# Expert scores of a mixture layer: one slab of each pair from whole float32 operands, the other in three passes

## The chip, the cores and the metric

The kernel runs on one core of a Trainium2 chip. Its time is the device time of one execution in microseconds; the figure quoted is the median of several runs. Engines are named as in the profile: PE is TensorE (PEld its weight loads), DVE is VectorE, ACT is ScalarE, POOL is GpSimd, and SP is SyncE, which issues the loads.

## The reference, cut to what matters

Two model blocks run one after the other, each with two layers, over 256 tokens of width 1024. The change lies in one part of the first block, the PEER layer, which runs once in each of its two layers: 16,384 experts, each one row of `u` and one row of `v`, of which every token takes 16 for each of 8 heads.

```python
def peer(xn, w_q, sub_keys, u, v):
    q = (xt @ w_q).astype(jnp.float32).reshape(t, PEER_HEADS, 2, PEER_HALF)
    sc = jnp.einsum('thpc,pnc->thpn', q, sub_keys.astype(jnp.float32))
    top_s, top_i = lax.top_k(sc, PEER_TOPK)
    cand = top_s[:, :, 0, :, None] + top_s[:, :, 1, None, :]
    best_s, best_c = lax.top_k(cand.reshape(t, PEER_HEADS, PEER_TOPK * PEER_TOPK), PEER_TOPK)
...
    expert = i1 * N_KEYS + i2
    gate = jax.nn.softmax(best_s, axis=-1)
...
        act = jax.nn.gelu(jnp.einsum('cd,chkd->chk', xc, u[ec]))
        return jnp.einsum('chk,chkd->cd', (gc * act).astype(xc.dtype), v[ec])
```

## The kernel before

`peer` (from L686) does not gather. It scores all 16,384 experts against all 256 tokens, multiplies by a gate that is zero for every expert not chosen, and sums the rows of `v`. The matrix `u` is streamed in 64 pairs of 256 rows; a pair is one raw tile of 1 MB, fetched by four loads of 256 KB that SP issues (`u_rows`), and has two slabs of 128 experts. DVE transposes a slab in blocks of 32 x 32, and PE multiplies it with the normalized tokens `xs` (eight tiles of 128 x 256).

There are two ways to multiply. In `u_whole` a slab is transposed out of the raw tile into a tile `ut` (L894) and multiplied as float32 in 8 products (L898; each leaves two records in the trace). In `u_split` it is transposed in place (L906); ACT copies a rounded half `whi` (L909), DVE subtracts it to get the rest `wlo` (L910), and `mm3` makes three passes for each of the 8 products (L198 to L200): high by high, high by low, low by high, with `xh` and `xl`, the halves of `xs`.

The order of the program is this. After two heads' scores, pair 0 is whole. Then a loop emits, for each pair, first the next pair's `u_whole`, then the gelu of the pair in hand (`u_out`), then four or five steps of other work: first `routing` (77 steps, nine a head, so two pairs a head), which computes the scores of heads 2 to 7 (product L762, whose weights are a further raw tile, and L772), finds the best 16 of each (L747 to L751, L789), adds up candidates (L800) and picks indices (L803, with POOL); then `spread_gates` (64 steps, 16 pairs), which turns the chosen experts and gates into a dense gate: DVE makes a one-hot `oh` (L859), `eq` (L861) and `rhs` (L863) for four tokens, PE multiplies them (L868), DVE or ACT puts the result into `act` (L872). After 37 whole pairs a layer come the other 27, as `u_split`, interleaved with the 64 pairs of `v`.

A scheduler sets the order on each engine by priority. `K.ahead()`, which is `high_priority(offset=600)`, moves what stands in it, here loads and transposes, forward in that order. Three kinds of ring tile matter, with three buffers each: `raw` (the loads of `u`, of the query weights and of `v` share it), `whi` and `wlo`. In `u_whole` the two `ut` tiles of a pair take one buffer of `whi` and one of `wlo`.

Of the kernel before, what the change touches and what calls it, by code (L numbers as in the profile page):

```python
# [12 lines left out]
F32 = mybir.dt.float32  # L13
F32R = mybir.dt.float32r
# [10 lines left out]
S = 256  # L25
KT = 8
# [642 lines left out]
def steps(gen, n):  # L669
    for _ in range(n):  # L670
        if next(gen, None) is None and gen.gi_frame is None:
            return
# [13 lines left out]
def peer(K, a, l, pre, xg, row, pool, ctx):  # L686
# [8 lines left out]
    tc, nc = K.tc, K.nc  # L695
# [36 lines left out]
    rrow = scratch([128, S])  # L732
    with tc.high_priority(offset=URGENT):
        nc.scalar.activation(rrow, row, AF.Copy)
    xs = Tiles([K.x_tile(KT + m, F32) for m in range(KT)])
    for m in range(KT):
        nc.vector.tensor_tensor(xs[:, m], xg[:, m], rrow, ALU.mult)
    skT = scratch([128, 2, 128])
# [2 lines left out]
    ps = K.ax_ps()  # L741
# [11 lines left out]
    def head_scores(hd):  # L753
        qs, sc = qs_b[hd % 2], sc_b[hd % 2]
        with K.ahead():
            raw = K.raw_tile().rearrange("p (k f) -> p k f", k=KT)
            K.rows_in(raw, a["w_peer_q"][l][:, hd * 256:hd * 256 + 256])
        x = xg if hd < 2 else xs
        ps = K.ax_ps().rearrange("p (m t) -> p m t", m=2)
        for k in range(KT):  # L760
            for m in range(2):
                nc.tensor.matmul(ps[:, m], raw[:, k, m * 128:m * 128 + 128], x[:, k], start=k + m == 0,  # L762
                                 stop=k == KT - 1 and m == 1)
        if hd < 2:
            nc.vector.tensor_tensor(qs, ps, rrow[:, None, :].to_broadcast([128, 2, S]), ALU.mult)
        else:
            nc.scalar.activation(qs, ps, AF.Copy)
        p2 = K.ax_ps()
        for tb in range(2):
            for s in range(2):  # L770
                i = 2 * tb + s
                nc.tensor.matmul(p2[:, i * 128:i * 128 + 128], qs[:, s, tb * 128:tb * 128 + 128],  # L772
                                 skT[:, s], start=True, stop=True)
        nc.scalar.activation(sc, p2.rearrange("p (i n) -> p i n", i=4), AF.Copy)
# [71 lines left out]
    def spread_gates():  # L846

        for i, t0 in enumerate(range(0, S, GT)):
            tag = "gab"[i % 3]
            pg = K.g_ps() if tag == "g" else K.ax_ps(tag)
            pg = pg.rearrange("p (t n) -> p t n", n=128)
            ts = slice(t0, t0 + GT)
            tok = lambda x: x[:, None, ts].to_broadcast([128, 128, GT])
            oh = pool.tile([128, 128, GT], FP16, name="oh", tag="oh", bufs=2)
            nc.vector.tensor_tensor(oh, io4, tok(mT), ALU.is_equal)  # L859
            eq = pool.tile([128, 128, GT], FP16, name="eq", tag="eq", bufs=1)  # L860
            nc.vector.tensor_tensor(eq, io4, tok(nT), ALU.is_equal)  # L861
            rhs = pool.tile([128, 2, 128, GT], FP16, name="rhs", tag="rhs", bufs=4)
            nc.vector.tensor_tensor(rhs, eq[:, None].to_broadcast([128, 2, 128, GT]),  # L863
                                    gp[:, :, None, ts].to_broadcast([128, 2, 128, GT]), ALU.mult)
            with tc.high_priority(offset=GPRIO):
                for t in range(GT):
                    for part in range(2):
                        nc.tensor.matmul(pg[:, t], oh[:, :, t], rhs[:, part, :, t], start=t + part == 0,  # L868
                                         stop=t == GT - 1 and part == 1)
            pg = pg.rearrange("p t n -> p n t")  # L870
            n = made[0]
            nc.vector.scalar_tensor_tensor(act[:, :n, ts], act[:, :n, ts], 1.0 / GSCALE, pg[:, :n],  # L872
                                           op0=ALU.mult, op1=ALU.mult)
            nc.scalar.activation(act[:, n:, ts], pg[:, n:], AF.Copy, scale=1.0 / GSCALE)
            spread[0] = t0 + GT
            yield
# [3 lines left out]
    def u_rows(b):  # L880

        raw = K.raw_tile().rearrange("p (j f) -> p j f", j=8)
        src = u[b * 256:b * 256 + 256].rearrange("(j r) d -> r j d", r=32)
        for pb in range(4):
            K.dma(raw[pb * 32:pb * 32 + 32], src[:, :, pb * 256:pb * 256 + 256])
        return [raw[:, jh * 4:jh * 4 + 4].rearrange("p j (k c) -> p k j c", k=KT) for jh in range(2)]

    def u_whole(b):
        turned = []
        with K.ahead():  # L890
            for jh, blk in enumerate(u_rows(b)):
                tag = ("whi", "wlo")[jh]
                turned.append(K.ring.tile([128, KT, 4, 32], F32, name="ut", tag=tag, bufs=3))
                nc.vector.transpose(turned[jh], blk)  # L894
        ps = K.mm_ps().rearrange("p (m t) -> p m t", m=2)
        for jh in range(2):
            for k in range(KT):
                nc.tensor.matmul(ps[:, jh], turned[jh][:, k].rearrange("p j c -> p (j c)"), xs[:, k],  # L898
                                 start=k + jh == 0, stop=k == KT - 1 and jh == 1)
        return ps  # L900

    def u_split(b):
        halves = []
        with K.ahead():
            for blk in u_rows(b):
                nc.vector.transpose(blk, blk)  # L906
                hi = K.ring.tile([128, KT, 4, 32], F32R, name="whi", tag="whi", bufs=3)
                lo = K.ring.tile([128, KT, 4, 32], F32R, name="wlo", tag="wlo", bufs=3)
                nc.scalar.activation(hi, blk, AF.Copy)  # L909
                nc.vector.tensor_tensor(lo, blk, hi.bitcast(F32), ALU.subtract)  # L910
                halves.append((hi, lo))
        ps = K.mm_ps().rearrange("p (m t) -> p m t", m=2)
        for jh, (hi, lo) in enumerate(halves):
            for k in range(KT):
                K.mm3(ps[:, jh], hi[:, k].rearrange("p j c -> p (j c)"), lo[:, k].rearrange("p j c -> p (j c)"),
                      xh[:, k], xl[:, k], k == 0 and jh == 0, k == KT - 1 and jh == 1)
        return ps

    def u_out(b, ps):

        t = spread[0]
        av = act[:, 2 * b:2 * b + 2]
        if t:
            nc.scalar.activation(ps[:, :, :t], ps[:, :, :t], AF.Gelu_apprx_tanh)
            nc.vector.tensor_tensor(av[:, :, :t], ps[:, :, :t], av[:, :, :t], ALU.mult)
        if t < S:
            nc.scalar.activation(av[:, :, t:], ps[:, :, t:], AF.Gelu_apprx_tanh)  # L927
        made[0] = 2 * b + 2
# [17 lines left out]

    for hd in range(2):
        head_scores(hd)
    ps, b = u_whole(0), 0
    for work, count in ((routing(), ROUTING_STEPS), (spread_gates(), SWEEP_STEPS)):  # L950
        while work.gi_frame is not None:
            nxt = u_whole(b + 1)
            u_out(b, ps)
            ps, b = nxt, b + 1
            steps(work, count(b))
    nxt = u_whole(b + 1)
    u_out(b, ps)
    ps, b = nxt, b + 1
    xh, xl = Tiles([]), Tiles([])
    for m in range(KT):  # L960
        xh.tiles.append(K.x_tile(2 * m))
        xl.tiles.append(K.x_tile(2 * m + 1) if m < KT - 1 else
                        pool.tile([128, S], F32R, name="xl", tag="oh", bufs=2))
        K.split_act(xh[:, m], xl[:, m], xs[:, m])
    u_out(b, ps)
    b += 1
    K.wide = 1
# [2 lines left out]
    for i in range(64):  # L970
        v_pair(i)
        if b < 64 and i >= (b - first) * U_AFTER:
            u_out(b, u_split(b))
            b += 1
    K.wide = K.nmm = 0
    return out
# [846 lines left out]

# [10 lines left out]
```

## Time and profile before

| | |
|---|---|
| median of 3 runs | 3681.95 us (3676.75 to 3683.27) |
| the profiled execution | 3676.36 us, its span 3674.6 us |
| PE, PEld | 3520.1 us (96%), 3241.4 us (88%) |
| DVE, ACT, POOL | 2620.0 us (71%), 1476.0 us (40%), 610.8 us (17%) |
| mean granted clock of PE | 0.976 of full speed |
| read from HBM | 530.39 MB |

The shares are of the span of one execution, and are averages over stages with different limits. In the two layers the stages that the change touches lie at about 413 to 615 us and 1750 to 1955 us (`routing`), and 617 to 797 us and 1955 to 2140 us (`spread_gates`). The rest of the span is other work of the two blocks, and the stage in which `u_split` and the pairs of `v` run.

### The profile page before, as it was taken

The numbers are of one execution on the slowest core, as the hardware profiler recorded it, in microseconds if no ns is written. First come the engines' busy times: TensorE is split into PE (matmuls) and PEld (weight loads), VectorE is DVE, ScalarE is ACT, GpSimd is POOL, SyncE is SP. The second block draws the span as 40 slices with busy tenths as digits, with TensorE's granted clock in tenths as the row PEclk, the third lists the DMA queues.
The fourth block names the chain that finished last, engine by engine and source line by source line (L and its number), as shares of the span: only waits on it lengthen the run. The fifth ranks groups of instructions, "written<-read, shape, count | busy, mean of one in ns | idle before, by whom it ended". The sixth has DMA issues, their size and how long they took to land. (4 is left out here: it accounts for less than half of the span.)

```text
span 3674.6 us, 60192 instructions
## 1 busy us (share of the span) xinstructions
PE 3520.1 (96%) x23381; PEld 3241.4 (88%) x23381; DVE 2620.0 (71%) x4704; ACT 1476.0 (40%) x2418; POOL 610.8 (17%) x583
## 2 busy tenths in 40 slices
PE   8899999999999999999999999999989999999999
PEld 8898887888888889998888888888888999989999
DVE  6966658876666657775668866666568777698875
ACT  6555211224444446454112134444445344444433
POOL 1200111000000002101121000000033543345441
PEclk9999999999999999999999999999999999999999
DMA  8885766436666567866766446666577544666433
GB/s 172 176 179 138 159 133 134 100 90 184 180 181 180 193 170 159 185 153 148 149 133 120 103 116 182 184 184 185 194 163 139 108 95 103 163 133 124 92 94 117
DMA packets 433976, 541.70 MB, mean 147 GB/s; under 512 B 28665, under 2 KB 392219, under 8 KB 432667
## 3 DMA queue, kind: packets, MB, share of 16 engines
q1 hardware_dynamic: 433690, 537.86, 62.9%
q8 instruction: 183, 3.00, 0.4%
q14 instruction: 103, 0.84, 0.1%
HBM read 530.39 MB, written 6.32 MB: 146 GB/s over the span
## 5 line engine op out<-in xcount | busy, mean ns | idle before, releaser
L170 DVE TENSOR_TENSOR wlo<-raw,whi 128x1024 fp32r<-128x1024 f32 x670 | 861.7, 1291 | 339.2 <-ACT whi L167 323.5
L167 ACT ACTIVATE whi<-raw 128x1024 fp32r<-128x1024 f32 x696 | 728.8, 1051 | 735.7 <-PE mm L199 272.2
L898 PE MATMUL mm<-x,ut 128*128 128x256 f32 x2368 | 546.1, 388 | 1.2 <-ACT act L927 1.2
L200 PE MATMUL mm<-x,wlo 128*128 128x256 f32 x1760 | 509.1, 289 | 11.3 <-DVE wlo L170 11.1
L898 PEld LDWEIGHTS mm<-x,ut 128*128 128x128 f32 x2368 | 455.6, 196 | 65.4 <-ACT act L927 3.7
L198 PE MATMUL mm<-x,whi 128*128 128x256 f32 x1760 | 507.2, 288 | 3.6 <-ACT whi L167 3.6
L199 PE MATMUL mm<-x,whi 128*128 128x256 f32 x1708 | 492.2, 288 | 0.0
L200 PE MATMUL gg<-x,wlo 128*128 128x256 f32 (+1 forms) x1456 | 416.1, 286 | 9.8 <-DVE wlo L170 9.8
L198 PE MATMUL gg<-x,whi 128*128 128x256 f32 (+1 forms) x1456 | 416.3, 286 | 5.7 <-ACT whi L167 5.7
L199 PE MATMUL gg<-x,whi 128*128 128x256 f32 x1400 | 399.0, 285 | 1.0 <-DVE x L303 1.0
L200 PEld LDWEIGHTS mm<-x,wlo 128*128 128x128 f32 x1760 | 342.4, 195 | 14.7 <-DVE wlo L170 13.8
L198 PEld LDWEIGHTS mm<-x,whi 128*128 128x128 f32 x1760 | 342.7, 195 | 10.5 <-issue 5.3
L943 PE MATMUL ax<-wlo,ah 128*128 128x512 f32 x1024 | 318.8, 392 | 20.3 <-DVE wlo L170 20.3
L199 PEld LDWEIGHTS mm<-x,whi 128*128 128x128 f32 x1708 | 332.2, 195 | 1.7 <-issue 0.7
L943 PE MATMUL ax<-whi,al 128*128 128x512 f32 x1024 | 316.7, 391 | 0.0
L200 PEld LDWEIGHTS gg<-x,wlo 128*128 128x128 f32 (+1 forms) x1456 | 280.0, 192 | 11.5 <-DVE wlo L170 11.1
L198 PEld LDWEIGHTS gg<-x,whi 128*128 128x128 f32 (+1 forms) x1456 | 280.1, 192 | 9.1 <-ACT whi L167 6.6
L943 PE MATMUL ax<-whi,ah 128*128 128x512 f32 x1024 | 281.5, 391 | 0.0
L894 DVE STREAM_TRANSPOSE ut<-raw 128x1024 f32<-128x1024 f32 x148 | 182.1, 1237 | 138.1 <-DMA raw<-in_peer_u_dram 111.6
L199 PEld LDWEIGHTS gg<-x,whi 128*128 128x128 f32 x1400 | 269.2, 192 | 2.9 <-DVE x L303 1.1
L943 PEld LDWEIGHTS ax<-wlo,ah 128*128 128x128 f32 x1024 | 190.8, 188 | 68.3 <-DVE wlo L170 29.4
L906 DVE STREAM_TRANSPOSE raw<-raw 128x1024 f32<-128x1024 f32 x108 | 128.1, 1224 | 159.6 <-DMA raw<-in_peer_u_dram 159.6
(534 smaller groups left out, 6705.1 us busy)
## 6 DMA issues: line engine op xcount, KB each, us to landing
raw<-in_w_in_dram SPq DMA_DIRECT2D x592, 256.0 KB
raw<-in_peer_u_dram SPq DMA_DIRECT2D x512, 256.0 KB
raw<-in_peer_v_dram SPq DMA_DIRECT2D x128, 1024.0 KB
raw<-in_w_branch_dram SPq DMA_DIRECT2D x16, 1024.0 KB
raw<-in_w_out_dram SPq DMA_DIRECT2D x16, 1024.0 KB
raw<-in_w_peer_q_dram SPq DMA_DIRECT2D x64, 256.0 KB
raw<-in_w_in_dram SPq DMA_DIRECT2D x64, 128.0 KB
raw<-in_w_branch_dram SPq DMA_DIRECT2D x32, 256.0 KB
```

What stands on the lines that cost most here:

```text
L167: nc.scalar.activation(view(hi), src, AF.Copy)
L170: (nc.gpsimd if pool else nc.vector).tensor_tensor(view(lo), src, view(hi).bitcast(F32), ALU.subtract)
L198: t.matmul(out, wh, xh, start=start, stop=False)
L199: t.matmul(out, wh, xl, start=False, stop=False)
L200: t.matmul(out, wl, xh, start=False, stop=stop)
L894: nc.vector.transpose(turned[jh], blk)
L898: nc.tensor.matmul(ps[:, jh], turned[jh][:, k].rearrange("p j c -> p (j c)"), xs[:, k], start=k + jh == 0, stop=k == KT - 1 and jh == 1)
L906: nc.vector.transpose(blk, blk)
L943: nc.tensor.matmul(out[tb][c], lhs[:, j, ts], r[:, c * 512:c * 512 + 512], start=b + j == 0 and lhs is ah and r is vh, stop=b == 63 and j ...
```

## The change

`u_whole` and `u_split` become one function `u_pair(b, whole)`, in which `whole` says which slabs of the pair are multiplied whole. Pair 0 stays whole. The pairs of the loop, 35 a layer, have slab 0 whole (transposed into a tile of the tag `whi`) and slab 1 in three passes, with transpose in place and both halves. The last pair ahead of the `v` stage is in three passes altogether, and the 27 others are as before. In all, 37 slabs a layer go from whole to three passes.

With this `xh` and `xl` are made ahead of the loop, and `xs` moves to eight tiles of its own (16 to 23), since the tiles that it used hold halves now; the 8 KB that this takes in each partition are paid by the tile that held the last `xl` and by a smaller scratch for dynamic DMA.

```diff
-    xs = Tiles([K.x_tile(KT + m, F32) for m in range(KT)])
+    xs = Tiles([K.x_tile(2 * KT + m, F32) for m in range(KT)])
...
+    def u_pair(b, whole=()):
+
+        parts = []
         with K.ahead():
-            for jh, blk in enumerate(u_rows(b)):
-                tag = ("whi", "wlo")[jh]
-                turned.append(K.ring.tile([128, KT, 4, 32], F32, name="ut", tag=tag, bufs=3))
-                nc.vector.transpose(turned[jh], blk)
...
+            for j, blk in enumerate(u_rows(b)):
+                if j in whole:
+                    t = K.ring.tile([128, KT, 4, 32], F32, name="ut", tag="wlo" if j in whole[1:] else "whi", bufs=3)
+                    nc.vector.transpose(t, blk)
+                    parts.append((t,))
+                    continue
                 nc.vector.transpose(blk, blk)
                 hi = K.ring.tile([128, KT, 4, 32], F32R, name="whi", tag="whi", bufs=3)
                 lo = K.ring.tile([128, KT, 4, 32], F32R, name="wlo", tag="wlo", bufs=3)
                 nc.scalar.activation(hi, blk, AF.Copy)
                 nc.vector.tensor_tensor(lo, blk, hi.bitcast(F32), ALU.subtract)
+                parts.append((hi, lo))
         ps = K.mm_ps().rearrange("p (m t) -> p m t", m=2)
+        for j, part in enumerate(parts):
             for k in range(KT):
+                w = [x[:, k].rearrange("p j c -> p (j c)") for x in part]
+                start, stop = k + j == 0, k == KT - 1 and j == 1
+                if j in whole:
+                    nc.tensor.matmul(ps[:, j], w[0], xs[:, k], start=start, stop=stop)
+                else:
+                    K.mm3(ps[:, j], *w, xh[:, k], xl[:, k], start, stop)
         return ps
...
-    ps, b = u_whole(0), 0
+    ps, b = u_pair(0, (0, 1)), 0
+    xh, xl = K.new_xs()
+    for m in range(KT):
+        K.split_act(xh[:, m], xl[:, m], xs[:, m])
     for work, count in ((routing(), ROUTING_STEPS), (spread_gates(), SWEEP_STEPS)):
         while work.gi_frame is not None:
-            nxt = u_whole(b + 1)
+            nxt = u_pair(b + 1, (0,))
             u_out(b, ps)
             ps, b = nxt, b + 1
             steps(work, count(b))
-    nxt = u_whole(b + 1)
+    nxt = u_pair(b + 1)
...
-            u_out(b, u_split(b))
+            u_out(b, u_pair(b))
...
-    nc = _bacc.Bacc("TRN2", target_bir_lowering=False, num_devices=1, dynamic_dma_scratch_size=8192)
+    nc = _bacc.Bacc("TRN2", target_bir_lowering=False, num_devices=1, dynamic_dma_scratch_size=4096)
```

Two places in DVE's order show what moves. The first lies in the middle of the spread of layer 0. In the kernel before, DVE has this there; `ut` are the slabs transposed out of a raw tile, `gg`, `ax` and `mm` are results of PE, and `DMAHW` in a wait stands for the four loads of a raw tile. The tile raw_7393 takes the place of raw_7102, which ut_7109 was the last to read, 42 rows ahead of ut_7398.

```order
L894 STREAM_TRANSPOSE ut_7303<-raw_7296 128x1024 [waits PE_49]
L872 SCALAR_TENSOR_TENSOR act_4652<-act_4652,gg_7034 128x62x4 [waits Activation_49]
L861 TENSOR_TENSOR eq_7088<-io4_4655,nT_4658 128x512 [waits DVE_49]
L872 SCALAR_TENSOR_TENSOR act_4652<-act_4652,ax_7051 128x62x4 [waits PE_49]
L859 TENSOR_TENSOR oh_7086<-io4_4655,mT_4657 128x512
L863 TENSOR_TENSOR rhs_7090<-eq_7088,gp_4659 128x1024 [waits DVE_49]
L861 TENSOR_TENSOR eq_7134<-io4_4655,nT_4658 128x512 [waits DVE_49]
L894 STREAM_TRANSPOSE ut_7398<-raw_7393 128x1024 [waits DMAHW6_49,DMAHW5_49,DMAHW7_49,DMAHW0_49,PE_49]
```

In the changed kernel the same stage reads like this on DVE; raw_7491 takes the place of raw_7143.

```order
L902 TENSOR_TENSOR wlo_7152<-raw_7143,whi_7151 128x1024 [waits Activation_49]
L861 TENSOR_TENSOR eq_7112<-io4_4655,nT_4658 128x512 [waits DVE_49]
L921 TENSOR_TENSOR act_4652<-mm_6923,act_4652 128x2x112 [waits Activation_49]
L859 TENSOR_TENSOR oh_7110<-io4_4655,mT_4657 128x512 [waits PE_49]
L863 TENSOR_TENSOR rhs_7114<-eq_7112,gp_4659 128x1024 [waits DVE_49]
L895 STREAM_TRANSPOSE ut_7264<-raw_7259 128x1024 [waits PE_49]
L859 TENSOR_TENSOR oh_7127<-io4_4655,mT_4657 128x512 [waits PE_49]
L872 SCALAR_TENSOR_TENSOR act_4652<-act_4652,ax_7075 128x52x4 [waits Activation_49]
L872 SCALAR_TENSOR_TENSOR act_4652<-act_4652,ax_7092 128x52x4
L861 TENSOR_TENSOR eq_7129<-io4_4655,nT_4658 128x512 [waits DVE_49]
L863 TENSOR_TENSOR rhs_7131<-eq_7129,gp_4659 128x1024 [waits DVE_49]
L898 STREAM_TRANSPOSE raw_7491<-raw_7491 128x8x4x32 [waits DMAHW3_49,DMAHW4_49,DMAHW2_49,DMAHW1_49]
```

The last read of the old tile, a subtraction now, and the first touch of the tile that takes its place stand 11 rows apart instead of 42.

The second place is the choosing of experts, again on DVE. Before, around the first pair of a head in layer 0:

```order
L894 STREAM_TRANSPOSE ut_5330<-raw_5325 128x1024 [waits DMAHW6_49,DMAHW5_49,DMAHW7_49,DMAHW0_49,PE_49]
L800 TENSOR_TENSOR act_4652<-act_4652 128x864 [waits Activation_49]
L800 TENSOR_TENSOR act_4652<-act_4652 128x864
L894 STREAM_TRANSPOSE ut_5332<-raw_5325 128x1024 [waits PE_49]
L803 TENSOR_REDUCE act_4652<-act_4652 128x16 [waits Pool_49] x2
L894 STREAM_TRANSPOSE ut_5374<-raw_5369 128x1024 [waits DMAHW3_49,DMAHW2_49,DMAHW4_49,DMAHW1_49,PE_49]
```

And in the changed kernel, around a pair whose load (raw_5421) the subtraction wlo_5260 releases, 13 rows ahead:

```order
L749 MATCH_REPLACE act_4652<-act_4652 128x128 [waits DVE_49] x3
L750 MAX act_4652<-act_4652 128x8 [waits DVE_49] x4
L751 MAX_INDEX act_4652<-act_4652 128x8 [waits DVE_49]
L898 STREAM_TRANSPOSE raw_5421<-raw_5421 128x8x4x32 [waits DMAHW6_49,DMAHW7_49,DMAHW5_49,DMAHW0_49]
L751 MAX_INDEX act_4652<-act_4652 128x8 [waits DVE_49] x2
L789 TENSOR_TENSOR act_4652<-act_4652 128x2x8
L751 MAX_INDEX act_4652<-act_4652 128x8 [waits DVE_49]
L789 TENSOR_TENSOR act_4652<-act_4652 128x2x16
L902 TENSOR_TENSOR wlo_5367<-raw_5358,whi_5366 128x1024 [waits Activation_49]
L895 STREAM_TRANSPOSE ut_5426<-raw_5421 128x1024 [waits PE_49]
```

Here the in-place transpose stands first among the steps of the pair, ahead of the subtraction of the pair before and of the other slab's own transpose.

## Rows read from the trace of the kernel before

**Rows 1.** The page: span; engines' busy time; groups by busy time, mean ns, idle.

```profile
span 3674.6 us, 60192 instructions
...
PE 3520.1 (96%) x23381; PEld 3241.4 (88%) x23381; DVE 2620.0 (71%) x4704; ACT 1476.0 (40%) x2418; POOL 610.8 (17%) x583
...
L170 DVE TENSOR_TENSOR wlo<-raw,whi 128x1024 fp32r<-128x1024 f32 x670 | 861.7, 1291 | 339.2 <-ACT whi L167 323.5
...
L894 DVE STREAM_TRANSPOSE ut<-raw 128x1024 f32<-128x1024 f32 x148 | 182.1, 1237 | 138.1 <-DMA raw<-in_peer_u_dram 111.6
```

**Rows 2.** Windows by stage: length, busy us (instructions) per engine, clock, DMA share, GB/s.

```profile
413.00:615.00 202.00, 191.30 (x895) 167.22 (x893) 142.38 (x513) 27.81 (x62) 42.64 (x56) 0.98 0.75 144
617.00:797.00 180.00, 174.49 (x1010) 153.54 (x1009) 148.93 (x303) 38.05 (x95) 0.00 (x0) 0.96 0.44 91
...
1955.00:2140.00 185.00, 176.99 (x1014) 155.31 (x1013) 155.02 (x313) 38.74 (x99) 0.27 (x1) 0.95 0.45 93
```

**Rows 3.** Windows of 20 us in the spread, columns (PE, PEld, DVE, ACT, POOL) alike.

```profile
660.00:680.00 20.00, 20.00 (x120) 18.06 (x119) 16.58 (x36) 4.91 (x12) 0.00 (x0) 1.00 0.46 93
...
760.00:780.00 20.00, 15.85 (x88) 13.09 (x87) 16.22 (x31) 3.80 (x11) 0.00 (x0) 0.91 0.40 96
```

**Rows 4.** Timeline of PE, choosing: start, us, engine, line, operands, count [idle <-releaser].

```profile
503.25 7.07 PE L762 MATMUL ax<-x,raw 128*128 128x256 f32 x32
...
524.87 7.07 PE L762 MATMUL ax<-x,raw 128*128 128x256 f32 x32
```

**Rows 5.** Timeline of SP's queue and of DVE, choosing and the first one-hot.

```profile
454.92 1.79 SPq L95 DMA_DIRECT2D raw<-in_w_peer_q_dram  x4
...
467.37 2.37 DVE L894 STREAM_TRANSPOSE ut<-raw 128x1024 f32<-128x1024 f32 x2 [10.22 <-DMA raw<-in_peer_u_dram]
...
490.00 1.25 DVE L894 STREAM_TRANSPOSE ut<-raw 128x1024 f32<-128x1024 f32 x1 [3.32 <-DMA raw<-in_peer_u_dram]
...
563.51 1.25 DVE L894 STREAM_TRANSPOSE ut<-raw 128x1024 f32<-128x1024 f32 x1 [3.22 <-DMA raw<-in_peer_u_dram]
...
617.18 0.72 DVE L859 TENSOR_TENSOR oh<-io,mT 128x512 f16<-128x512 f16 x2
```

**Rows 6.** Timeline of PE: three-pass products ahead of the layer; whole slabs and spreading products.

```profile
388.30 0.28 PE L198 MATMUL ax<-bh,whi 128*128 128x256 f32 x1
...
390.34 0.28 PE L200 MATMUL ax<-bh,wlo 128*128 128x256 f32 x1
...
642.45 5.79 PE L898 MATMUL mm<-x,ut 128*128 128x256 f32 x26
648.08 2.05 PE L868 MATMUL ax<-rhs,oh 128*128 128x128 f16 x16
649.95 1.48 PE L898 MATMUL mm<-x,ut 128*128 128x256 f32 x6
```

**Rows 7.** Timeline of DVE in the spread.

```profile
640.79 1.25 DVE L894 STREAM_TRANSPOSE ut<-raw 128x1024 f32<-128x1024 f32 x1 [0.29 <-PE mm L898]
...
661.05 0.42 DVE L859 TENSOR_TENSOR oh<-io,mT 128x512 f16<-128x512 f16 x1
...
662.04 0.69 DVE L863 TENSOR_TENSOR rhs<-eq,gp 128x1024 f16<-128x1024 f16 x1
662.65 0.34 DVE L872 SCALAR_TENSOR_TENSOR act<-act,ax 128x184 f32<-128x184 f32 x1
...
673.89 1.25 DVE L894 STREAM_TRANSPOSE ut<-raw 128x1024 f32<-128x1024 f32 x1
```

**Rows 8.** Timeline of SP's queue, DVE and PE at the end of the spread.

```profile
761.86 1.79 SPq L95 DMA_DIRECT2D raw<-in_peer_u_dram  x4
...
769.22 2.37 DVE L906 STREAM_TRANSPOSE raw<-raw 128x1024 f32<-128x1024 f32 x2 [3.46 <-DMA raw<-in_peer_u_dram]
...
774.01 1.11 PE L868 MATMUL ax<-rhs,oh 128*128 128x128 f16 x8 [2.31 <-DVE oh L859]
776.74 1.11 PE L868 MATMUL gg<-rhs,oh 128*128 128x128 f16 x8 [1.62 <-DVE rhs L863]
```

**Rows 9.** Line L894: idle of DVE ahead of it, by releaser (us, times).

```profile
  PE mm L898: 26.0, 33
```

More of the change, by code (lines that the diff above doesn't have):

```diff
@@ L886, in u_rows @@
         return [raw[:, jh * 4:jh * 4 + 4].rearrange("p j (k c) -> p k j c", k=KT) for jh in range(2)]
-    def u_whole(b):
-        turned = []
+    def u_pair(b, whole=()):
+        parts = []
         with K.ahead():
-            for jh, blk in enumerate(u_rows(b)):
-                tag = ("whi", "wlo")[jh]
-                turned.append(K.ring.tile([128, KT, 4, 32], F32, name="ut", tag=tag, bufs=3))
-                nc.vector.transpose(turned[jh], blk)
[L895 to L905, printed above, removed]
+            for j, blk in enumerate(u_rows(b)):
[4 more added lines that the diff above has]
+                    continue
                 nc.vector.transpose(blk, blk)
@@ L910, in u_split @@
                 nc.vector.tensor_tensor(lo, blk, hi.bitcast(F32), ALU.subtract)
-                halves.append((hi, lo))
+                parts.append((hi, lo))
         ps = K.mm_ps().rearrange("p (m t) -> p m t", m=2)
-        for jh, (hi, lo) in enumerate(halves):
+        for j, part in enumerate(parts):
             for k in range(KT):
-                K.mm3(ps[:, jh], hi[:, k].rearrange("p j c -> p (j c)"), lo[:, k].rearrange("p j c -> p (j c)"),
-                      xh[:, k], xl[:, k], k == 0 and jh == 0, k == KT - 1 and jh == 1)
+                w = [x[:, k].rearrange("p j c -> p (j c)") for x in part]
[4 more added lines that the diff above has]
+                    K.mm3(ps[:, j], *w, xh[:, k], xl[:, k], start, stop)
         return ps
@@ L955, in peer @@
             steps(work, count(b))
-    nxt = u_whole(b + 1)
+    nxt = u_pair(b + 1)
     u_out(b, ps)
     ps, b = nxt, b + 1
[L959 to L964, printed above, removed]
     u_out(b, ps)
```

## Prediction

> **What bounds the kernel now.** I read first the page: TensorE (PE) is busy 96% of the span, VectorE (DVE) 71% [rows 1]. A share over the whole span says little about two stages, so the windows come next. While experts are chosen (413 to 615 us) PE is busy 191.30 of 202.00 us and DVE 142.38; while gates are spread (617 to 797) PE 174.49 of 180.00 and DVE 148.93; layer 1 has the spread again from 1955 to 2140 with nearly the same figures [rows 2]. Inside the spread PE has no gap in 660 to 680, and at its end, 760 to 780, 15.85 of 20 us [rows 3]. So the spread is bound by PE, with DVE close behind at 83%.
>
> The choosing is not bound by PE. One head costs PE 21.62 us, the distance of two query products (503.25 and 524.87) [rows 4]. DVE goes round more slowly: the first transpose of every second pair begins only when its rows have landed, at 490.00 and, three heads on, at 563.51, so 73.51 / 3 = 24.5 us for a head, each time after 3.2 us or more of idle DVE [rows 5]. PE lives there on an early lead. The end of this stage, the first one-hot at 617.18 [rows 5], is set by loads and DVE.
>
> **What the change takes away.** In the timeline of PE 26 fp32 records of a whole slab take 648.08 - 642.45 = 5.63 us, .2165 each, and a slab has 16: 3.46 us [rows 6]. Passes stand .12 us apart (17 steps from 388.30 to 390.34) [rows 6], and a slab has 24: 2.88 us. That is .58 us a slab. 35 mixed pairs and both slabs of the last make 37 slabs a layer, 74 in all: 43 us less PE work. That is the whole gain, if PE stays the bound.
>
> **What it adds on DVE and ACT.** The split slab's transpose in place costs DVE what the old one cost (1237 ns [rows 1]). New is its subtraction, 1291 ns [rows 1], once a pair. A pair of the spread takes (673.89 - 640.79) / 3 = 11.0 us now [rows 7], so 180 us hold 16.4 pairs and DVE works 148.93 / 16.4 = 9.1 us in each. With the subtraction it has 10.4 us, still under 11.0. ACT gets a copy of about a microsecond and has room. The splits of xs, moved ahead, add nothing: they are the same sixteen operations, and in the order they already ran ahead of the routing. Moving xs to other tiles and halving the DMA scratch touches no engine's time that I can see; I take nothing.
>
> **What it moves: when a raw tile comes free.** There are three raw tiles. Before, one was free when its second transpose out of it was done, and the next transpose that needs the refilled tile stood far down DVE's order (in the piece shown, the load behind ut_7398 was released by ut_7109, 42 rows ahead). Now the split slab is transposed inside the raw tile, and the tile is held until the subtraction has read it. In the piece shown wlo_7152 releases the tile and the transpose of its refill raw_7491 is only 11 rows behind it. It is alike in all 13 pairs that I followed in the spread: 5.0 to 6.1 us of DVE work by the durations of the rows (one-hot .42, right-hand side .69, gate product .34, whole transpose 1.25 [rows 7]).
>
> How long does a tile need? At 761.86 SP issues a load as soon as DVE has let the tile go, and the transposes that wait for it begin at 769.22: 7.36 us [rows 8]. So DVE reaches the transpose 1.3 to 2.4 us early and stands there, with one-hots and right-hand sides behind it for which PE waits. The old trace shows this very picture once a layer: DVE idle 3.46 us, then PE idle 2.31 and 1.62 us for oh and rhs [rows 8].
>
> The wait closes a circle, once a pair: landing 7.4, transpose 1.2, and what DVE has between this transpose and the subtraction that frees the next tile, 1.5 to 6.5 us, mean 4.6 over ten pieces of the order. 7.4 + 1.2 + 4.6 = 13.2 us instead of 11.0. 13 pairs by 2.2 are 29 us; some 3 to 4 of the idle that stands at the end already [rows 8] are in that. **Spread: +26 us a layer.** PE has 3.46 + 2.88 us of slabs and 32 spreading products (.117 each, 16 from 648.08 to 649.95 [rows 6], 3.7 us) in such a pair, 10.1 us, and waits 3; its gain is gone. Around 760 to 780, with 4 us of PE idle, the clock is granted at .91 [rows 3]; 10.1 / .91 = 11.1 is still under 13.2, so I give the clock no term.
>
> The Trainium skill, in DMA: Bandwidth & Descriptors, section Specifications, puts HBM at about 358 GB/s for a core and the first byte at 0.6 us on the sync path. By that a tile of 1.05 MB would be there in an estimated 3.5 us, ahead of every one of the transposes; the row's 7.36 us disagree. What this would make of the sum is the third rival.
>
> **The choosing.** The same circle, longer: per head two pairs and a query tile. Landing 7.4; from the transpose through the second subtraction 3.4 (the piece around raw_5421); then a query tile and a U tile queued one behind the other, which took from the issue at 454.92 to the transposes at 467.37, 12.5 us [rows 5]; transpose and subtraction 2.5. Sum 25.8 against 24.5 before: 1.3 a head, 8 us over six heads. More comes at the start, where DVE is crowded and each of the first loads now waits for a subtraction instead of a transpose. I placed the new order's rows one behind the other with these durations and landings: the query tile issued at 454.92 before comes at about 473, the last one about 32 us late, the first one-hot at about 653 instead of 617.18. **Choosing: +36 us a layer.** This is the softest term. Its bounds: nothing, if the lead of the loads at the start is kept, and 50, if the circle is worse by a further wait of about 2 us a head. The order puts 36 nearer to the upper end.
>
> **Sum.** 3676.4 us (the profiled execution; its span is 3674.6 [rows 1]) + 2 x (36 + 26) = 3800.4, taken as 3800. The median of the runs shown is 5.6 above that execution, inside their spread.
>
> **The rivals.** *PE stays the bound.* If no wait of DVE reached PE, the 43 us would come out: 3676 - 43 = 3633. For it speaks the page's 96%; against it, that the choosing was never PE's, and the 7.36 us.
>
> *Only the spread pays.* The choosing absorbs the later loads, because PE's lead and DVE's idle of 3 to 4 us before each late transpose [rows 5] give room. Then 3676 + 52 = 3728.
>
> *The refill lands in time (ends on the other side).* If a load that goes alone landed in under 5.0 us, the in-place transpose would never wait. A pair of the spread then falls from 11.0 to DVE's 10.4: 16 x .6 x 2 = 19 us less, the choosing unchanged: about 3657. It decides at the 5.0 us of DVE work between release and transpose; the one clean row, 7.36, is against it.
>
> *The halves ring bites too.* The tag whi now carries two buffers a pair instead of one, at three buffers. Already before, transposes waited for PE to let a buffer go, 26.0 us in 33 times, .8 each [rows 9]. If both uses in 70 pairs paid as much, 2 x 70 x .8 = 112, less the 26 there now, 86 on top: 3886. Against it: a PE that waits for DVE has let its buffers go early.
>
> *The change doesn't do what it says*, that is, the order keeps its lead in spite of the code: the order shows the moved rows, so I give that nothing.
>
> **How the numbers follow.** Loop in both stages, 3800: .57. Spread alone, 3728: .21. Ring too, 3886: .09. In time, 3657: .08. PE bound, 3633: .05. The range leaves out the two fast cases (.13) and half of the last slow one: 3705 to 3860, which takes in the 0 to 50 us a layer of the choosing (3728 to 3828) with a margin for the size of the circle. A measurement of this kernel tells about 0.2%, 7 us, from no change. Slower: .87; faster: the two fast cases less a little, .11; same: .02.
>
> **What would show it.** Right: in the spread, DVE idle before the in-place transpose, released by the load, about 2 us in 13 pairs, PE idle about 3 us a pair and pairs 13 us apart; the first one-hot at about 650; passes at .12. Wrong: DVE waits there for ACT's copy or for PE more than for loads; pairs at 10 to 11 us; landings of 4 to 5 us once only one tile is on its way, which would sink the forecast at once.

## The result, and the profile after

The changed kernel takes 3802.53 us (median of 4 runs, 3799.58 to 3805.22) against 3679.35 us of the kernel before on the same chip: a ratio of 1.0343, 95% interval 1.0321 to 1.0365. The profiled execution has a span of 3797.8 us, 123.2 more than before.

Cut at the starts of three kinds of instruction in the traces (first query product, first one-hot, first product with `v`, last product with `v`), the loss lies where the change is, in both layers (us):

| | choosing | spread | stage of `v` |
|---|---|---|---|
| before, layer 0 and 1 | 220.9, 221.3 | 181.6, 183.3 | 528.3, 522.9 |
| after | 256.7, 259.7 | 210.5, 212.9 | 519.2, 519.3 |
| difference | +35.8, +38.4 | +28.9, +29.6 | -9.1, -3.6 |

These add up to 120; some 3 us lie elsewhere.

The page of the changed kernel, span, engines and two of the groups; it answers to [rows 1]. L898 is now the transpose in place, the idle ahead of it stands behind the second bar.

```profile
span 3797.8 us, 61648 instructions
...
PE 3532.8 (93%) x23973; PEld 3268.6 (86%) x23973; DVE 2699.3 (71%) x4778; ACT 1549.2 (41%) x2492; POOL 610.0 (16%) x583
...
L200 PE MATMUL mm<-x,wlo 128*128 128x256 f32 x2352 | 695.3, 296 | 73.3 <-DVE wlo L902 62.7
...
L898 DVE STREAM_TRANSPOSE raw<-raw 128x1024 f32<-128x1024 f32 x182 | 219.9, 1232 | 348.4 <-DMA raw<-in_peer_u_dram 348.3
```

DVE stands 348 us ahead of in-place transposes, nearly all of it for loads of `u`. Before, the 108 in-place transposes of the `v` stage waited 159.6 us, as this line of that page has it, and the transposes out of the tile 111.6 [rows 1].

```profile
L906 DVE STREAM_TRANSPOSE raw<-raw 128x1024 f32<-128x1024 f32 x108 | 128.1, 1224 | 159.6 <-DMA raw<-in_peer_u_dram 159.6
```

Note PE: 43 us of work were taken away by the prediction's count, yet it is busy for 12.7 us more.

The windows by stage of the changed kernel (columns as in [rows 2]):

```profile
413.00:651.00 238.00, 197.83 (x1076) 180.11 (x1074) 164.16 (x532) 49.71 (x87) 46.13 (x56) 0.92 0.63 122
651.00:860.00 209.00, 180.86 (x1147) 160.40 (x1148) 167.01 (x324) 56.62 (x115) 0.00 (x0) 0.88 0.37 79
```

Neither engine is full any more: in the spread PE is busy 87% and DVE 80%, where before PE had 97% [rows 2]. The granted clock is .92 and .88, where it was .98 and .96.

The same windows split the loss on DVE. In the choosing (413 to 615 before, 413 to 651 now) DVE is busy for 21.8 us more and idle for 14.2 more; in the spread (617 to 797, 651 to 860) busy for 18.1 more and idle for 10.9 more. So well over half of the added time is DVE's own added work, and the rest waiting. Whether that work would cost as much without the wait, the windows can't say; a run below does.

Now the circle, in the timeline of DVE in the spread of the changed kernel (start, us, instruction, in brackets the idle ahead of it and its releaser), and between them the queue of SP:

```profile
674.01 1.22 DVE L902 TENSOR_TENSOR wlo<-raw,whi 128x1024 fp32r<-128x1024 f32 x1
...
682.66 1.25 DVE L898 STREAM_TRANSPOSE raw<-raw 128x1024 f32<-128x1024 f32 x1 [2.31 <-DMA raw<-in_peer_u_dram]
684.97 1.22 DVE L902 TENSOR_TENSOR wlo<-raw,whi 128x1024 fp32r<-128x1024 f32 x1
...
693.91 1.25 DVE L898 STREAM_TRANSPOSE raw<-raw 128x1024 f32<-128x1024 f32 x1 [3.42 <-DMA raw<-in_peer_u_dram]
...
700.25 1.22 DVE L902 TENSOR_TENSOR wlo<-raw,whi 128x1024 fp32r<-128x1024 f32 x1
701.49 10.84 SPq L95 DMA_DIRECT2D raw<-in_peer_u_dram  x6
...
708.81 1.25 DVE L898 STREAM_TRANSPOSE raw<-raw 128x1024 f32<-128x1024 f32 x1 [2.37 <-DMA raw<-in_peer_u_dram]
...
776.41 1.22 DVE L902 TENSOR_TENSOR wlo<-raw,whi 128x1024 fp32r<-128x1024 f32 x1
```

The subtraction that begins at 700.25 frees its tile, SP issues the refill at 701.49, and the transpose begins at 708.81, after 7.32 us; the two turns above give 7.4 and 7.7 from the end of the subtraction. Each time DVE has stood 2.3 to 3.4 us. Eight turns take 776.41 - 674.01 = 102.4 us, 12.8 each, where a pair took 11.0 [rows 7].

### The profile page after: what moved, and what is told of

Read it like the earlier page. It is cut to its first block, busy times and chain, and to the rows that moved or that the text cites. A ratio compares the mean times of both kernels' runs of the same rounds, so it can differ in the third digit from the quotient of the medians.

```text
span 3797.8 us, 61648 instructions
## 1 busy us (share of the span) xinstructions
PE 3532.8 (93%) x23973; PEld 3268.6 (86%) x23973; DVE 2699.3 (71%) x4778; ACT 1549.2 (41%) x2492; POOL 610.0 (16%) x583
## 5 line engine op out<-in xcount | busy, mean ns | idle before, releaser
L167 ACT ACTIVATE whi<-raw 128x1024 fp32r<-128x1024 f32 x696 | 728.8, 1051 | 731.8 <-PE mm L199 282.5
L200 PE MATMUL mm<-x,wlo 128*128 128x256 f32 x2352 | 695.3, 296 | 73.3 <-DVE wlo L902 62.7
L198 PE MATMUL mm<-x,whi 128*128 128x256 f32 x2352 | 704.3, 299 | 2.9 <-ACT whi L167 2.5
L199 PE MATMUL mm<-x,whi 128*128 128x256 f32 x2352 | 689.1, 293 | 0.0
L200 PEld LDWEIGHTS mm<-x,wlo 128*128 128x128 f32 x2352 | 471.0, 200 | 81.3 <-DVE wlo L902 67.4
L198 PEld LDWEIGHTS mm<-x,whi 128*128 128x128 f32 x2352 | 470.4, 200 | 11.7 <-issue 5.3
L199 PEld LDWEIGHTS mm<-x,whi 128*128 128x128 f32 x2352 | 470.0, 200 | 3.5 <-issue 0.7
L898 DVE STREAM_TRANSPOSE raw<-raw 128x1024 f32<-128x1024 f32 x182 | 219.9, 1232 | 348.4 <-DMA raw<-in_peer_u_dram 348.3
L198 PE MATMUL gg<-x,whi 128*128 128x256 f32 (+1 forms) x1456 | 416.6, 286 | 5.2 <-ACT whi L167 5.2
L199 PE MATMUL gg<-x,whi 128*128 128x256 f32 (+1 forms) x1456 | 415.2, 285 | 1.0 <-DVE x L303 1.0
L910 PE MATMUL mm<-x,ut 128*128 128x256 f32 x1184 | 300.6, 411 | 25.7 <-ACT act L923 25.7
L901 ACT ACTIVATE whi<-raw 128x1024 fp32r<-128x1024 f32 x182 | 192.4, 1057 | 319.9 <-PE ax L939 104.6
L910 PEld LDWEIGHTS mm<-x,ut 128*128 128x128 f32 x1184 | 241.4, 209 | 67.0 <-ACT act L923 31.5
L198 PEld LDWEIGHTS gg<-x,whi 128*128 128x128 f32 (+1 forms) x1456 | 280.4, 193 | 8.3 <-ACT whi L167 5.8
L199 PEld LDWEIGHTS gg<-x,whi 128*128 128x128 f32 (+1 forms) x1456 | 280.3, 193 | 2.9 <-DVE x L303 1.1
```

Source lines behind the costliest of these rows:

```text
L167: nc.scalar.activation(view(hi), src, AF.Copy)
L198: t.matmul(out, wh, xh, start=start, stop=False)
L199: t.matmul(out, wh, xl, start=False, stop=False)
L200: t.matmul(out, wl, xh, start=False, stop=stop)
L910: nc.tensor.matmul(ps[:, j], w[0], xs[:, k], start=start, stop=stop)
```

## The experiments

Theory A is the one of the prediction: the raw tile is held until the subtraction, the refill lands over 7 us later, and DVE reaches the in-place transpose sooner. Theory B says that the price is DVE's added work, wherever the tile is freed. Theory C puts it on what goes along with the change.

**One stage at a time.**

```diff
-            nxt = u_pair(b + 1, (0,))
+            nxt = u_pair(b + 1, (0,) if count is SWEEP_STEPS else (0, 1))
```

> The changed kernel, but the pairs that run while experts are chosen are whole again; only the pairs of the spread stay mixed. Theory A (a raw tile is held until the subtraction, its refill lands 7.4 us later, and the in-place transpose stands too close behind it in DVE's queue, so a circle of load, transpose and subtraction sets the pace): what the spread alone costs, 29 us a layer by the two traces (first one-hot to first product with v grew from 181.6 to 210.6 us), so 3680 + 58 = 3738. Theory B (the cost is DVE's added work, one subtraction of 1.22 us a pair, wherever the tile is freed): 32 pairs by 1.22 = 39, so 3719. Theory C (the cost comes from what goes along: xs in other tiles, the smaller scratch, the early halves of xs): 3800, unchanged.

Measured: 3770.95 us, ratio 1.0258 (1.0241 to 1.0275), against 3681.76 of the kernel before: 89 us more. For the other stage:

```diff
-            nxt = u_pair(b + 1, (0,))
+            nxt = u_pair(b + 1, (0,) if count is ROUTING_STEPS else (0, 1))
```

> The changed kernel, but the pairs of the spread are whole again; only the pairs that run while experts are chosen stay mixed. Theory A: the choosing alone costs 34 us a layer by the two traces (first one-hot 617.2 to 651.3), so 3680 + 68 = 3748, and e1 and this one add up to the whole loss. Theory B: 38 pairs by 1.22 = 46, so 3726. Theory C: 3800.

Measured: 3735.81 us, ratio 1.0155 (1.0137 to 1.0173), 54 us more. The first number is far above both theories (58 and 39). The second lies nearer to B's 46 than to A's 68: its interval is 50 to 64 us. So A's halves were wrong, these two runs don't decide between A and B, and 89 + 54 = 143 is 20 more than both stages together cost.

Cut at the same places, the first kernel has a choosing of 230.3 and 229.5 us and a spread of 220.3 and 223.3; the second has 247.1 and 246.2, then 182.8 and 183.5. So each stage loses when it alone has the mixed pairs. The losses of the choosing add up to no more than that of the changed kernel (9.4 + 26.2 = 35.6 us against 35.8 in layer 0, 33.1 against 38.4 in layer 1). The 20 us lie in the spread of the first kernel, which is 9.8 and 10.4 us longer than in the changed kernel. Between the first one-hot and the first product with `v` 13 mixed pairs have their in-place transpose there, where the changed kernel has 12, and its other four mixed pairs reach back into the choosing: one more turn of the circle falls into its spread, which fits the 10 us.

**What goes along.** All 37 pairs whole, the rest of the change kept:

```diff
-            nxt = u_pair(b + 1, (0,))
+            nxt = u_pair(b + 1, (0, 1))
...
-    nxt = u_pair(b + 1)
+    nxt = u_pair(b + 1, (0, 1))
```

> The changed kernel with both slabs of all 37 pairs whole again: only the moved xs, the smaller scratch and the early halves of xs are left of the change. Theories A and B: as the kernel before, 3672 to 3688. Theory C: near 3800.

Measured: 3681.22 us, ratio 1.0000 (0.9986 to 1.0014). Theory C is out: the moved `xs`, the smaller scratch and the early halves cost nothing that shows, and the interval is 5 us to either side.

**The tile freed early.** The same instructions on every engine, but the split slabs of the loop's pairs and of the last pair go to tiles of their own:

```diff
-                nc.vector.transpose(blk, blk)
+                t = K.ring.tile([128, KT, 4, 32], F32, name="ut", tag="wlo", bufs=3) if early else blk
+                nc.vector.transpose(t, blk)
+                blk = t
```

> The changed kernel, but the split slab of the loop's pairs is transposed out of the raw tile into a tile of the tag wlo, and halved from there, so that the raw tile is free after its two transposes as in the kernel before; DVE, ACT and PE do the same instructions. Theory A: the circle is gone, DVE no longer waits for loads in the spread, and part of PE's 43 us comes back: 3640 to 3665. Theory B: DVE's work is unchanged, so 3790 to 3810. A third possibility, that the wlo ring with two tiles a pair becomes the wait: in between, 3700 to 3780, with DVE waiting for PE ahead of the transposes.

Measured: 3664.37 us, ratio 0.9959 (0.9942 to 0.9975), 17 us less than before and 138 less than the changed kernel, with the same DVE work. That is theory A, and B falls. The third possibility falls too: no transpose of the pairs is listed as waiting for PE. The choosing takes 206.8 and 210.4 us, shorter than before by 14.1 and 10.9; the spread 186.3 and 192.6, longer by 4.7 and 9.3. Windows of this kernel show why, one in the choosing, one in the spread (columns as in [rows 2]):

```profile
480.00:500.00 20.00, 20.00 (x120) 18.39 (x119) 17.18 (x59) 5.20 (x9) 5.32 (x7) 1.00 0.82 157
...
680.00:700.00 20.00, 19.01 (x132) 17.43 (x131) 19.57 (x40) 6.31 (x13) 0.00 (x0) 1.00 0.49 106
```

In this window of the choosing PE is full, at full clock, so it gets the gain of the passes. DVE is busy there as long as in the changed kernel (175.8 us from the first query product to the first one-hot of layer 0, against 175.0), but idle for 31.0 us instead of 81.7: the added subtractions lengthened the choosing only as a part of the circle. In the window of the spread DVE is busy 19.57 of 20 us, but over the stage 90%, with PE at 92%; that the added subtraction is what makes the spread longer here is likely and not shown. Line L899 of this kernel, its transpose out of and into the tile, with the idle ahead of it:

```profile
  DMA raw<-in_peer_u_dram: 154.6, 55
```

55 waits, where the in-place transposes of the `v` stage before had 54: of the 74 new ones a single one waits, for .2 us.

**Half a tile to wait for.** The changed kernel again, hold and order kept, but in the spread (from pair 21 of a layer on) the split slab's rows are loaded first and by themselves:

```diff
+            if halves:
+                K.dma(raw[pb * 32:pb * 32 + 32, 4:8], src[:, 4:8, pb * 256:pb * 256 + 256])
+            else:
+                K.dma(raw[pb * 32:pb * 32 + 32], src[:, :, pb * 256:pb * 256 + 256])
+        for pb in range(4 * halves):
+            K.dma(raw[pb * 32:pb * 32 + 32, 0:4], src[:, 0:4, pb * 256:pb * 256 + 256])
```

> The changed kernel, with one difference: the mixed pairs of the spread load their two slabs separately, four loads of 128 KB for the split slab first, then four for the whole slab. The place of the transpose in DVE's order and the moment that frees the tile stay where they were (11 rows apart in the piece that I followed). Theory A (the circle of load, transpose, subtraction): the in-place transpose waits for half a tile only; by half of 7.4 us plus what does not shrink, an estimated 4 to 5 us, it lands within the 5.0 to 6.1 us of DVE work, and most of the 29 us a layer that the spread lost come back: 3745 to 3770. Theory B (DVE's added work is the price): unchanged, 3795 to 3810.

Measured: 3753.72 us, ratio 1.0232 (1.0213 to 1.0251), on a chip whose kernel before took 3669.15: 85 us lost where the changed kernel lost 123. The spread takes 193.3 us in both layers, 17 and 20 less than in the changed kernel; the choosing stays at 254.7 and 257.3. DVE's timeline in the spread of this kernel, where L903 is the transpose in place and L907 the subtraction:

```profile
671.03 1.22 DVE L907 TENSOR_TENSOR wlo<-raw,whi 128x1024 fp32r<-128x1024 f32 x1
...
676.83 1.24 DVE L903 STREAM_TRANSPOSE raw<-raw 128x1024 f32<-128x1024 f32 x1
680.25 1.22 DVE L907 TENSOR_TENSOR wlo<-raw,whi 128x1024 fp32r<-128x1024 f32 x1
...
686.13 1.25 DVE L903 STREAM_TRANSPOSE raw<-raw 128x1024 f32<-128x1024 f32 x1 [0.82 <-DMA raw<-in_peer_u_dram]
...
757.04 1.23 DVE L907 TENSOR_TENSOR wlo<-raw,whi 128x1024 fp32r<-128x1024 f32 x1
```

From the end of a subtraction (681.47) to the transpose it is 4.66 us now, of which DVE waits .82; in the turn before it comes 4.58 us behind and DVE doesn't wait at all. Eight pairs take 86.0 us, 10.75 each. Over the whole spread DVE waits 7.9 and 10.1 us ahead of these transposes, where it waited 34.7 and 34.4 in the changed kernel. The landing time is what the circle of the spread hung on.

The spread is still 12 and 10 us longer than before, and no longer by waiting: in layer 0 DVE is idle for 23.9 us of it, less than the 31.5 before, and busy for 19 more.

**The version that beats both.** From the kernel that frees the tile early, with the spread whole as before:

```diff
-            nxt = u_pair(b + 1, (0,), True)
+            nxt = u_pair(b + 1, (0,) if count is ROUTING_STEPS else (0, 1), True)
```

> The pairs that run while experts are chosen are mixed, with the split slab transposed out of the raw tile as in the kernel that freed it early; the pairs of the spread are whole, as in the kernel before. Theory A: the choosing keeps its gain of 14 and 11 us in the two layers, the spread has its old 182 and 183 us instead of 186 and 193, so 3664 - 14 = 3650, within 3640 to 3660. Theory B: the added subtractions of the choosing would have cost 46, so 3726.

Measured: 3641.06 us, ratio 0.9918 (0.9901 to 0.9934): .8%, or 28 us, faster than the kernel before on the chip of the half-load run. The choosing takes 205.9 and 209.4 us, the spread 178.0 and 176.8, a few us less than it ever had; no run tells why.

**The subtraction on POOL.** From the kernel that frees the tile early, in the spread:

```diff
-                nc.vector.tensor_tensor(lo, blk, hi.bitcast(F32), ALU.subtract)
+                (nc.gpsimd if early and b > 20 else nc.vector).tensor_tensor(lo, blk, hi.bitcast(F32), ALU.subtract)
```

> The kernel that frees the tile early, with the subtraction of the spread's pairs moved from DVE to POOL, which is idle there (a subtraction on POOL took 2.4 us elsewhere in the trace). If DVE's 94% in the spread of that kernel is what holds it there, 1.22 us a pair less bring the spread from 186 and 193 us to 172 to 180: 3640 to 3650. If POOL and DVE hinder each other, or the longer subtraction holds PE up, 3664 to 3690.

Measured, on that chip too: 3660.41 us, ratio 0.9973 (0.9959 to 0.9988), against 0.9959 with the subtraction on DVE; the spread takes 192.3 and 189.9 us, no better than with the subtraction on DVE. POOL's subtractions and what DVE ran beside them, in the timelines of this kernel:

```profile
664.83 2.40 POOL L904 TENSOR_TENSOR wlo<-ut,whi 128x1024 fp32r<-128x1024 f32 x1 [13.44 <-ACT whi L903]
665.28 2.23 DVE L859 TENSOR_TENSOR oh<-io,mT 128x512 f16<-128x512 f16 x1
...
674.90 2.86 POOL L904 TENSOR_TENSOR wlo<-ut,whi 128x1024 fp32r<-128x1024 f32 x1 [7.66 <-ACT whi L903]
675.54 2.50 DVE L861 TENSOR_TENSOR eq<-io,nT 128x512 f16<-128x512 f16 x1
```

A one-hot of .42 us takes 2.23 and ends .28 us after POOL's subtraction; an `eq` takes 2.50 and ends .28 us after the next. It is so beside 29 of the 34 subtractions on POOL: what DVE runs there takes over 1 us longer than the same instructions in the kernel that frees the tile early, and 1.6 us on average over all 34, where 1.22 was saved. What leaves DVE comes back as longer instructions of DVE. The Trainium skill says so in SBUF — State Buffer, section Who interferes with whom: a DVE instruction with two SBUF inputs contends with a GpSimd instruction that reads SBUF, for a pair of ports that is "an exclusive lock"; these rows agree.

## Why the prediction was right

3800 was forecast, 3802.53 measured, and the two stages lost what they were to lose, by the waits that were named. That the sum is within 3 us is luck in part: the spread lost 58.5 us in the two layers instead of 52, the stage of `v`, which had no term, gave 12.7 back, and 3 us lie elsewhere.

The choosing: +36 a layer forecast, +35.8 and +38.4 measured. The query tiles are issued in the changed kernel at these times, in SP's queue:

```profile
446.02 1.79 SPq L95 DMA_DIRECT2D raw<-in_w_peer_q_dram  x4
...
471.23 1.79 SPq L95 DMA_DIRECT2D raw<-in_w_peer_q_dram  x4
...
574.06 2.82 SPq L95 DMA_DIRECT2D raw<-in_w_peer_q_dram  x4
```

The second was forecast at 473 and comes at 471.23, where it was 454.92 [rows 5]; four heads take 102.8 us, 25.7 each, forecast 25.8. The last one was forecast about 32 us late and is 28.7 late against the kernel before:

```profile
545.38 1.93 SPq L95 DMA_DIRECT2D raw<-in_w_peer_q_dram  x4
```

The first one-hot was forecast at 653:

```profile
651.34 0.75 DVE L859 TENSOR_TENSOR oh<-io,mT 128x512 f16<-128x512 f16 x2
```

So the softest term was right by its parts: a circle a little longer than before, and most of the loss at the start. What the prediction doesn't say is that the subtractions it adds lie on this circle and are its larger part (21.8 us of 36, by the windows above).

The spread: +26 forecast, +28.9 and +29.6 measured. The circle was forecast at 13.2 us and is 12.8; the landing at 7.4 and is 7.3 to 7.7; DVE's wait ahead of the transpose at 1.3 to 2.4 and is 2.3 to 3.4 in the rows shown, so that the work between release and transpose is at most 4.3 to 5.1 us there, where 5.0 to 6.1 were counted. The circle, 13 pairs by 1.8, gives 23 us by these measured figures, and between the first and the sixteenth multiplication by the gate the spread did grow by 22.8 and 24.2 us. The other 6 us lie at its end: the first product with `v` begins 6.7 and 6.6 us behind that multiplication, where it was .9. The prediction took off 3 to 4 us there, and no run tells what holds it up.

What failed is small. The stage of `v` was given nothing and gained 9.1 and 3.6 us; no run tells why. And passes do not stand at .12 throughout, as the last part of the prediction says. In PE's timeline of the changed kernel, in the spread:

```profile
698.99 0.41 PE L200 MATMUL mm<-x,wlo 128*128 128x256 f32 x1
699.63 0.41 PE L200 MATMUL mm<-x,wlo 128*128 128x256 f32 x1
...
708.09 0.28 PE L200 MATMUL mm<-x,wlo 128*128 128x256 f32 x1
708.45 0.28 PE L200 MATMUL mm<-x,wlo 128*128 128x256 f32 x1
```

Third passes stand .64 us apart, .213 a pass, and nine us later .36, that is .12. The windows around them (columns as in [rows 2]) have the granted clock:

```profile
694.00:698.00 4.00, 2.25 (x18) 1.93 (x18) 3.90 (x8) 0.81 (x2) 0.00 (x0) 1.00 0.00 0
...
700.00:702.00 2.00, 2.00 (x12) 2.00 (x11) 2.00 (x4) 0.45 (x1) 0.00 (x0) 0.55 0.00 0
...
708.00:710.00 2.00, 2.00 (x20) 1.90 (x19) 1.19 (x2) 0.75 (x1) 0.00 (x0) 1.00 0.04 8
```

PE has stood for 1.75 of 4 us and then runs for some 3 us at the lower of its two clocks, 1.2 instead of 2.4 GHz. That is why it is busy longer with less to do. An estimate from the trace counts half of PE's busy time in the stretches granted .5 as lost: 129 us, where the kernel before lost 78. So the low clock adds 51 us, and what is left of PE's busy time falls by 38. I gave the clock no term because PE has time to spare in the circle. The half-load run fits this (its mean clock is .964, hardly above the .960 of the changed kernel, and it still got 38 us back), but no run took the clock away by itself, so its share of the loss stays open.

The rivals: *PE stays the bound* and *the refill lands in time* fell with the landing of 7.3 us, and the half-load run shows that the second was judged by the right quantity: at 4.66 us three quarters of the wait are gone. *Only the spread pays* fell with the choosing's 36 us. *The halves ring bites too* fell as well: among the changed kernel's transposes none is listed as waiting for PE, where before 33 did [rows 9].

## What to carry to other kernels

An operation that works in place holds its input buffer longer than one that works out of place, and when that buffer is a landing place for loads, the hold decides how far ahead the loads run. Compare two numbers: the work on the engine between the instruction that frees the buffer and the first instruction that needs its refill, and the time from issue to landing; when the first is smaller, the difference is paid on every turn, however idle the engines look, and so is work that is added to that engine within the turn. A copy that frees the buffer at once, from a ring that has room, can be worth more than the saved work itself.

## What the runs showed of the hardware

Two sizes of a load: a tile of 1.05 MB takes 7.32 us from issue to the waiting transpose, half of it, with the other half right behind it, about 4.66 from the release. The second half costs 2.66 us, which is an estimate of 197 GB/s, with some 2.0 us that don't shrink. The Trainium skill, in DMA: Bandwidth & Descriptors, section Anatomy of one DMA, gives about 2.0 us fixed and bytes by 436 GB/s for one DMA on the path through GpSimd. Here SP issues four loads, which alone takes 1.79 us [rows 8], so the 2.0 us can't be tested by these rows; of the rate they show less than half.

An idle POOL was no free place for two-input work beside a busy DVE: subtractions of 2.4 to 2.9 us on POOL cost DVE 1.6 us each on average.
